# Moving the dilated up-projection under attention, and the experts' weight subtractions from GpSimd to VectorE past routing, with 16-token marks

## The chip, the cores and the metric

One core of one Trainium2 chip. The metric is the time of one execution on the device in microseconds (us): the median of three runs of the same program. One further execution is taken by the hardware profiler, and all rows below come from it. Engines are written PE (TensorE, with PEld for its weight loads), DVE (VectorE), ACT (ScalarE), POOL (GpSimd) and SP (SyncE, which only issues transfers).

## What is computed

A stack of three layers over 512 tokens of 1024 features. The first block has an input projection, sparse attention (NSA) with three branches, dilated attention, two gates that merge them, and PEER, a layer of 16,384 small experts of which each token uses 128. Two hybrid layers with a feed-forward network follow; the change doesn't touch them. The part that matters, shortened:

```python
y_nsa = nsa_attention(...)
y_dil = dilated_attention(...)
gm = sigmoid(mg).reshape(B, S, 2, D)             # mg = h @ w_in[:, gate columns]
merged = gm[:, :, 0] * (y_nsa @ w_up_nsa) + gm[:, :, 1] * (y_dil @ w_up_dil)
x = x + merged @ w_o
# PEER: per token and head the 16 best of 128 keys in each of two halves, then the
# 16 best of the 256 sums; idx = e1 * 128 + e2 names an expert, g its softmax weight
a = einsum('cd,chkd->chk', xt, u[idx])
act = gelu(a) * g
x = x + einsum('chk,chkd->cd', act, v[idx])
```

## The kernel before

All products are of f32 data. A weight page (`WS.load`, 128 x 1024 f32, 512 KB) comes from DRAM on SP's queue into `wr`, is rounded by ACT into `wh` (L99), and `wl = wr - wh` is taken by `self.eng` (L100), VectorE or GpSimd. Each product is then three matmuls (`mm3`, L186 to L188): high by high, high by low, low by high. `wr`, `wh` and `wl` have three buffers each. Eight 128-column pieces make a page.

The order on each engine is worked out by a planner that simulates the program. It may move an instruction ahead of others on its engine unless an edge forbids that. `issue_after(ins)` puts what is traced in its block behind `ins` on the same engine; `keep_in_program_order` puts an instruction behind the one traced before it on its engine. While `self.pinned` is set, the matmuls of the expert loop stay in the traced order.

**Block 1.** `block1` projects the input, runs dilated attention (`dilated`, result `ydh`, `ydl`), normalises the heads (`head_norm`), transposes queries and keys (`to_fm`), compresses keys (`compress`) and runs `nsa`. The gates (`wmg`, 16 column tiles of one page each, evacuated by `evg` to `sg` and written to DRAM as `sig_d`) are traced after `nsa`, but the planner fills PE with them during it. The list `self.hold` says behind which ACT instruction the cast of each of their pages may run: the first four behind the last split of the keys (`start`), twelve behind softmax rows (`self.exps`) spread evenly. A held page has its subtraction on GpSimd. After that come the dilated up-projection `wupd` (2 pages, `ev1`, which loads the gate back from DRAM and writes `m`), the NSA up-projection `wupn` (4 pages, `ev2`) and the output projection `wo1`.

**PEER.** `peer` runs 128 experts' columns in two loops. Each "expert" e of the U loop is one page: 24 matmuls over 384 tokens into one bank, a GELU on ACT, and a transfer to DRAM (`a_d`, L1315) or, from e = RES on, a resident tile (`ares`, L1311). The remaining 128 tokens (TG) are served by gathering their 128 rows of u and of v one by one (`gather`: an indirect transfer issued by GpSimd, L1399, and a row product on VectorE, L1411 for u, L1425 for v).

Beside the U loop, generators are advanced by credits per expert. First `route` finds the experts of the tokens on VectorE: RT_C credits per expert. A tile of 128 tokens costs 41 credits, the whole 164 and a last RT_D. For each tile after the first, `finish` transposes its result on PE; it stands inside the next tile's work, after head h = 6 of the key search. After routing `build_g` builds the weights `g` of all 128 x 384 pairs: `marks` makes on VectorE four f16 tiles of TB tokens (`e1` L1555, `e2` L1557, two `og` L1561), PE multiplies them (L1578), ACT scales (L1580) and SP writes them to `g_d` (L1583). BG_C credits per expert are given to it, one for each yield. NU_C rows per expert are gathered during routing, during `build_g` and after it. In the U loop `wu.eng` is always GpSimd.

The V loop takes the experts in the order RES to 127, then from 0 up to RES: the product of activation and `g` (`at` or `ar` with `gt`, L1334), its split (`ah` L223, `al` L224) and 24 matmuls, with NV_C rows per expert beside it. Subtractions alternate between VectorE and GpSimd there.

Of the kernel before, what the change touches and what calls it, by code (L numbers as in the profile page):

```python
# [20 lines left out]
P = 128  # L21
S = 512
# [56 lines left out]
class WS:  # L79
# [7 lines left out]
    def load(self, p):  # L87
        if p not in self.have and p < self.ap.shape[0]:
# [6 lines left out]
            with ExitStack() as es:  # L95
                if self.b.hold:
                    es.enter_context(self.b.tc.issue_after(self.b.hold.pop(0)))
                    eng = nc.gpsimd
                nc.scalar.copy(hi, raw)  # L99
                eng.tensor_tensor(lo, raw, hi.bitcast(F32), OP.subtract)  # L100
# [15 lines left out]
class Builder:  # L116
# [705 lines left out]
    def to_fm(self, dst, src, scale=None):  # L822
# [6 lines left out]
        else:  # L829
            nc.scalar.mul(dst, p, scale)  # L830
# [4 lines left out]
    def block1(self):  # L835
# [81 lines left out]

        def ev1(t, p):
            nc.scalar.activation(zn[:, t, 8:12].rearrange("p h d -> p (h d)"), p[:, 0:256], AF.Copy,
                                 scale=r4[:, t:t + 1])  # L920
# [23 lines left out]
        for i in range(4):  # L944
            self.to_fm(qT[:, i], lambda t: zn[:, t, 2 * i:2 * i + 2].rearrange("p h d -> p (h d)"), 0.125)
        for i in range(2):
# [4 lines left out]
            for g in range(2):  # L951
                for u in range(2):
                    r = slice(u * 64, u * 64 + 64)
                    start = self.split(kT[0][r, 2 * i + g], kT[1 + u][r, 2 * i + g], p[g * 64:g * 64 + 64])
        self.compress(fs, kcT, vcm)
        ezn.close()

# [15 lines left out]
        m = sp.tile([P, KD, S], F32, name="m")  # L973
        mh = sp.tile([P, KD, S], F32R, name="mh")
        ml = sp.tile([P, KD, S], F32R, name="ml")

        def ev1(c, p):
            t = sp.tile([P, S], F32, tag="gt", name="gt", bufs=3)
            nc.sync.dma_start(t, sig_d[8 + c])
            nc.vector.scalar_tensor_tensor(m[:, c], t, 1.0, p, OP.add, OP.mult)  # L980
# [7 lines left out]
        self.lin(WS(self, self.a["wupd"]), 2, KD, (ydh, ydl), ev1)  # L988
# [22 lines left out]
    def compress(self, fs, kcT, vcm):  # L1011
        tc, nc = self.tc, self.nc
        with ExitStack() as es:
# [27 lines left out]
            nc.scalar.activation(ha, ph[:, 0:256], AF.Gelu_apprx_tanh)  # L1041
# [29 lines left out]
            nc.any.tensor_copy(vcm.rearrange("p g d -> p (g d)"), pv[:, 0:128])  # L1071

# [160 lines left out]
    def peer(self, src):  # L1233
# [5 lines left out]
        g_d = [self.dp.tile([P, NB, 16, NG], F32, tag=f"g_d{e}", name=f"g_d{e}") for e in range(8)]  # L1239
# [40 lines left out]
        for e in range(P):  # L1280
            if e == RES:
                assert routed and next(gen, None) is None
                gen = None
                ap = self.pool(es, "ares")
            wu.eng = nc.gpsimd
# [18 lines left out]
            for k in range(KD):  # L1304
                if routed and gen is not None and k in (2, 6) and credit >= 1.0:
                    next(gen, None)
# [494 lines left out]
```

## Time and profile before

| | |
|---|---|
| median of 3 runs | 3681.76 us (3679.64 to 3682.37) |
| the profiled execution | 3670.07 us |
| its span | 3668.3 us |
| PE busy in the span | 3497.4 us (95%) |
| DVE busy | 2303.4 us (63%) |
| ACT busy | 1397.4 us (38%) |
| POOL busy | 1111.2 us (30%) |

Matmuls are pipelined, and a busy PE is not PE at its peak: how far it is from its floor is read from the pace of its instructions. A window row gives the stretch, its length and, for each engine in the order PE, PEld, DVE, ACT, POOL, the busy time with the count of instructions that touch the stretch; then the granted share of PE's clock (1.00 is the upper of its two levels, 2.4 GHz), the busy share of the transfer engines and what they moved in GB/s. A waits row says who waited for whom, with the total in us, how often, and the longest. A row of a line gives the shortest, middle and longest duration in ns and the first and last start in us from the span's start. Block 1 lasts to about 584 us, the U loop from 634 to 1280, the V loop from there to 1876.

### The profile page before, as it was taken

What the parts mean: (1) busy time and instruction counts of PE and PEld (TensorE: products, weight loads), DVE (VectorE), ACT (ScalarE), POOL (GpSimd) and SP (SyncE); (2) the same over time, 40 slices, a digit from 0 to 9 for tenths busy, and PEclk for the clock granted to TensorE, in tenths of its full rate; (3) what the DMA queues carried; (4) which work ended last, traced back from release to release, by engine and by line L of the source; (5) the groups of instructions that cost most, each with busy time, mean ns of one, the idle gap of its engine ahead of it and who ended that gap; (6) DMA issues with size and microseconds to landing.
All of it is one profiled execution on the core that took longest, in us unless ns stands there. A gap on an engine that the chain in (4) does not pass through costs nothing.

```text
span 3668.3 us, 46596 instructions
## 1 busy us (share of the span) xinstructions
PE 3497.4 (95%) x17784; PEld 2968.8 (81%) x17784; DVE 2303.4 (63%) x3583; ACT 1397.4 (38%) x2159; POOL 1111.2 (30%) x637
## 2 busy tenths in 40 slices
PE   9979999999999899999999999999999999999998
PEld 7856668998999799888888768878887867778886
DVE  5354454999999699999975544554326363464433
ACT  5534433434665233323333443342223344233221
POOL 1002101666667786666620000231101000131100
PEclk9979999999999999999999999999999999999999
DMA  3212143565888999999952323433333333443332
GB/s 129 96 39 92 55 155 100 185 200 194 295 294 296 328 332 352 351 339 348 340 204 88 131 98 127 158 124 97 109 96 112 115 105 103 158 144 103 96 120 75
DMA packets 229016, 631.25 MB, mean 172 GB/s; under 512 B 22644, under 2 KB 57144, under 8 KB 228792
## 3 DMA queue, kind: packets, MB, share of 16 engines
q1 hardware_dynamic: 191928, 494.04, 39.9%
q0 software_dynamic: 36864, 134.23, 10.2%
q8 instruction: 139, 2.28, 0.3%
q14 instruction: 85, 0.70, 0.1%
HBM read 542.20 MB, written 85.98 MB: 171 GB/s over the span
## 4 chain that ended last, share of the span: by engine, by line
PE 71%; DVE 19%; issue 4%; DMA 2%; ACT 2%; POOL 1%; SPq 1%; ACTq 0%; DVEq 0%; POOLq 0%
PE ps L186 17%; PE ps L188 17%; PE ps L187 17%; PE v L186 3%; PE v L187 3%; PE v L188 3%; DVE og L1561 3%; PE o L415 2%; DVE nr L1411 2%; DVE e L1555 2%; PE s L392 2%; DMA wr<-in_pv 1%; PE tp L409 1%; DVE av L1425 1%; ACT wh L99 1%
## 5 line engine op out<-in xcount | busy, mean ns | idle before, releaser
L99 ACT CAST wh<-wr 128x1024 fp32r<-128x1024 f32 x599 | 626.6, 1050 | 1097.7 <-PE ps L187 741.2
L186 PE MATMUL ps<-hnh,wh 128*128 128x512 f32 (+1 forms) x2616 | 979.7, 378 | 16.2 <-ACT hnh L316 11.3
L188 PE MATMUL ps<-hnh,wl 128*128 128x512 f32 (+1 forms) x2616 | 978.4, 374 | 16.1 <-POOL wl L100 16.1
L187 PE MATMUL ps<-hnl,wh 128*128 128x512 f32 (+1 forms) x2616 | 976.7, 373 | 0.1
L100 POOL TENSOR_TENSOR wl<-wr,wh 128x1024 fp32r<-128x1024 f32 x215 | 562.5, 2618 | 699.7 <-ACT wh L99 592.4
L100 DVE TENSOR_TENSOR wl<-wr,wh 128x1024 fp32r<-128x1024 f32 x384 | 478.3, 1246 | 400.1 <-ACT wh L99 387.2
L186 PEld LDWEIGHTS ps<-hnh,wh 128*128 128x128 f32 x2616 | 498.1, 191 | 85.6 <-ACT hnh L316 12.2
L188 PEld LDWEIGHTS ps<-hnh,wl 128*128 128x128 f32 x2616 | 495.9, 190 | 87.5 <-POOL wl L100 19.6
L187 PEld LDWEIGHTS ps<-hnl,wh 128*128 128x128 f32 x2616 | 496.4, 190 | 67.0 <-DVE hnl L320 2.0
L186 PE MATMUL v<-ah,wh 128*128 128x384 f32 x1024 | 349.8, 342 | 44.9 <-ACT wh L99 44.7
L187 PE MATMUL v<-al,wh 128*128 128x384 f32 x1024 | 345.4, 338 | 0.0
L186 PEld LDWEIGHTS v<-ah,wh 128*128 128x128 f32 x1024 | 193.1, 189 | 57.2 <-ACT wh L99 56.4
L188 PE MATMUL v<-ah,wl 128*128 128x384 f32 x1024 | 228.3, 336 | 0.0
L1411 DVE SCALAR_TENSOR_TENSOR nr<-nr,xt 128x1024 f32<-128x1024 f32 x128 | 210.3, 1658 | 13.5 <-DMA nr<-in_ur,gx 13.5
L1425 DVE SCALAR_TENSOR_TENSOR av<-nr,na,av 128x1024 f32<-128x1024 f32 x127 | 211.4, 1665 | 1.6
L187 PEld LDWEIGHTS v<-al,wh 128*128 128x128 f32 x1024 | 193.3, 189 | 0.0
L675 POOL TENSOR_TENSOR sg<-sg,bcs 128x512 f32<-128x512 f32 x44 | 75.7, 1720 | 374.2 <-ACT sg L674 373.9
L1399 POOL DMA_INDIRECT nr<-in_ur,gx x128 | 176.0, 1375 | 39.7 <-issue 13.1
L188 PEld LDWEIGHTS v<-ah,wl 128*128 128x128 f32 x1024 | 182.9, 188 | 0.9 <-POOL wl L100 0.6
L625 POOL TENSOR_TENSOR gc<-gc,gy 128x512 f32<-128x512 f32 x16 | 24.2, 1513 | 522.6 <-DMA wr<-in_wb 237.8
L223 ACT CAST ah<-at 128x384 fp32r<-128x384 f32 x112 | 57.1, 512 | 328.0 <-DVE at L1334 224.6
L1399 POOL DMA_INDIRECT nr<-in_vr,gx x128 | 161.1, 1259 | 40.3 <-issue 19.0
(490 smaller groups left out, 5534.4 us busy)
## 6 DMA issues: line engine op xcount, KB each, us to landing
wr<-in_pu SPq DMA_DIRECT2D x128, 512.0 KB
wr<-in_pv SPq DMA_DIRECT2D x125, 512.0 KB
wr<-in_wgu SPq DMA_DIRECT2D x88, 512.0 KB
g_d<-gs SPq DMA_DIRECT2D x64, 384.0 KB
gt<-g_d SPq DMA_DIRECT2D x32, 768.0 KB
wr<-in_wgate SPq DMA_DIRECT2D x48, 512.0 KB
wr<-in_wdn SPq DMA_DIRECT2D x44, 512.0 KB
a_d<-ga SPq DMA_DIRECT2D x56, 384.0 KB
```

The source lines that it names most:

```text
L99: nc.scalar.copy(hi, raw)
L100: eng.tensor_tensor(lo, raw, hi.bitcast(F32), OP.subtract)
L186: self.pe(nc.tensor.matmul(out, w[0], x[0], start=start, stop=False))
L187: self.pe(nc.tensor.matmul(out, w[0], x[1], start=False, stop=False))
L188: self.pe(nc.tensor.matmul(out, w[1], x[0], start=False, stop=stop))
L392: nc.tensor.matmul(s[:, 0:n], q[:, t * P:n], k[:, 0:n], start=i == 0, stop=False)
L415: nc.tensor.matmul(o[j * 64:j * 64 + 64, b * P:S], heads[j][1](b), pts[j], start=first and b == 0, stop=last and b == NT - 1)
L675: nc.gpsimd.tensor_tensor(t, t, bc, OP.mult)
L1399: i = nc.gpsimd.indirect_dma_start(out=w[:], out_offset=None, in_=self.a[src], in_offset=bass.IndirectOffsetOnAxis(ap=self.near_i[:, j:j + ...
L1411: nc.vector.scalar_tensor_tensor(u, u, 1.0, xts[group[j]], OP.mult, OP.mult, accum_out=a[:, j:j + 1])
L1425: nc.vector.scalar_tensor_tensor(av, w, a[:, j:j + 1], av, OP.mult, OP.add)
L1561: nc.vector.tensor_tensor(o, e1, two(gT[:, i, tt]), OP.mult)
```

## The change

In block 1 the gate columns are packed so that those of the dilated branch come first. Their eight tiles are followed by the dilated up-projection, then by the eight tiles of the NSA gates; `m` moves to a pool that is open from before `nsa`, and `ev1` has its own two buffers `sd`. The list of holds names instructions from earlier on: `marks` holds ACT's last `zn` copy, the tanh of `gf`, the four `qT` copies, the last key split and the GELU of `compress`. There are seven such holds and eleven behind softmax rows, 18 for 18 pages.

In `peer` the subtraction of the U pages is VectorE's once routing is done. TB is 16, with two yields for each 16 tokens. `g_d` is laid out by groups of EG = 4 experts, in 12 blocks of 32 tokens: a write is 512-byte pieces, a read of `gt` one run of 6144 bytes per partition. Twenty experts are resident instead of 16. `build_g` may go on past RES. `finish` moves into the next tile's candidate search, and the row products of u are kept in program order. The credits are set anew.

```diff
             with ExitStack() as es:
-                if self.b.hold:
-                    es.enter_context(self.b.tc.issue_after(self.b.hold.pop(0)))
+                h = self.b.hold.pop(0) if self.b.hold else None
+                if h is not None:
+                    es.enter_context(self.b.tc.issue_after(h))
                     eng = nc.gpsimd
...
+            if t == NT - 1:
+                marks.append(i.ins)
...
-                nc.scalar.activation(gf, gf, AF.Tanh, scale=0.5)
+                marks.append(nc.scalar.activation(gf, gf, AF.Tanh, scale=0.5).ins)
...
-        self.compress(fs, kcT, vcm)
+        marks.append(i_split)
+        marks.append(self.compress(fs, kcT, vcm))
         ezn.close()
+        m = self.pool(er, "ym", side="right").tile([P, KD, S], F32, name="m")
...
-        self.hold = [start] * 4 + [self.exps[i * len(self.exps) // 12] for i in range(12)]
-        self.lin(WS(self, self.a["wmg"]), KD, 16, hn, evg)
+        self.hold = [marks[i] for i in (0, 0, 1, 3, 6, 6, 7)] + [self.exps[i * len(self.exps) // 11] for i in range(11)]
+        wmg = WS(self, self.a["wmg"])
+        self.lin(wmg, KD, KD, hn, lambda c, p: evg(KD + c, p))
+
+        def ev1(c, p):
+            t = gp.tile([P, S], F32, tag="sd", name="sd", bufs=2)
+            nc.sync.dma_start(t, sig_d[KD + c])
+            nc.vector.scalar_tensor_tensor(m[:, c], t, 1.0, p, OP.add, OP.mult)
+        self.lin(WS(self, self.a["wupd"]), 2, KD, (ydh, ydl), ev1)
+        self.lin(wmg, KD, KD, hn, evg)
         self.lin_tags = "bc"
...
-        self.lin(WS(self, self.a["wupd"]), 2, KD, (ydh, ydl), ev1)
         self.lin(WS(self, self.a["wupn"]), 4, KD, (ynh, ynl), ev2)
...
-        g_d = [self.dp.tile([P, NB, 16, NG], F32, tag=f"g_d{e}", name=f"g_d{e}") for e in range(8)]
+        g_d = [self.dp.tile([P, 16 // EG, NB, EG, NG], F32, tag=f"g_d{e}", name=f"g_d{e}") for e in range(8)]
...
             if e == RES:
-                assert routed and next(gen, None) is None
-                gen = None
-                ap = self.pool(es, "ares")
-            wu.eng = nc.gpsimd
+                assert routed
+                ap = self.pool(e2, "ares", side="right")
+            wu.eng = nc.vector if routed else nc.gpsimd
...
-                nc.sync.dma_start(gt, g_d[e // 16][:, :, e % 16:e % 16 + EG])
+                nc.sync.dma_start(gt, g_d[e // 16][:, e % 16 // EG])
...
-                nc.vector.scalar_tensor_tensor(u, u, 1.0, xts[group[j]], OP.mult, OP.mult, accum_out=a[:, j:j + 1])
+                self.tc.keep_in_program_order(
+                    nc.vector.scalar_tensor_tensor(u, u, 1.0, xts[group[j]], OP.mult, OP.mult,
+                                                   accum_out=a[:, j:j + 1]))
...
-                    if h == 6 and last is not None:
-                        finish(*last)
...
+                    if h == 4 and last is not None:
+                        finish(*last)
                     yield 1.5
...
+                    if h % 8 == 4 and h + 4 < TB:
+                        yield 1
                 if t0 + TB == NG:
                     for i in range(8):
-                        nc.sync.dma_start(g_d[i][:, tb], gs[:, 16 * i:16 * i + 16])
+                        nc.sync.dma_start(g_d[i][:, :, tb],
+                                          gs[:, 16 * i:16 * i + 16].rearrange("p (q e) t -> p q e t", e=EG))
...
-TB = 8
+TB = 16
-NB = 8
+NB = 12
-RES = 112
+RES = 108
-RT_D = 8.0
-RT_C = 3.2
-BG_C = 0.85
-NU_C = (0.4, 0.7, 2.0)
+RT_D = 14.0
+RT_C = 2.9
+BG_C = 0.78
+NU_C = (0.3, 1.15, 2.0)
```

## Rows read from the trace of the kernel before

**Rows 1.** The page's chain that ended last, shares of the span by engine

```profile
PE 71%; DVE 19%; issue 4%; DMA 2%; ACT 2%; POOL 1%; SPq 1%; ACTq 0%; DVEq 0%; POOLq 0%
```

**Rows 2.** Windows: an expert, an expert with a step of marks, a projection

```profile
637.96:642.12 4.16, 4.16 (x26) 4.16 (x26) 4.16 (x31) 2.83 (x3) 2.40 (x1) 1.00 0.01 2
...
926.50:931.65 5.15, 5.15 (x41) 4.99 (x41) 5.05 (x6) 3.51 (x4) 3.96 (x3) 1.00 0.88 285
...
520.00:540.00 20.00, 20.00 (x88) 16.13 (x87) 14.47 (x20) 6.58 (x9) 0.00 (x0) 1.00 0.42 142
```

**Rows 3.** Windows: busy us of PE PEld DVE ACT POOL, clock, DMA, GB/s

```profile
633.76:759.04 125.28, 125.28 (x747) 125.19 (x745) 125.04 (x558) 53.58 (x76) 75.77 (x35) 1.00 0.56 185
759.04:889.43 130.39, 118.14 (x660) 117.32 (x658) 129.53 (x344) 45.36 (x66) 85.02 (x39) 0.93 0.58 191
889.43:1182.35 292.92, 285.73 (x2114) 274.17 (x2113) 288.58 (x270) 179.49 (x208) 204.63 (x96) 1.00 0.81 285
1182.35:1280.17 97.82, 80.18 (x410) 76.02 (x409) 59.86 (x74) 24.91 (x36) 77.19 (x46) 0.93 0.93 328
...
1417.44:1876.00 458.56, 416.76 (x2319) 404.86 (x2319) 419.17 (x380) 140.93 (x193) 287.38 (x172) 0.99 0.93 336
```

**Rows 4.** TensorE's waits in U: total us, times, longest

```profile
PE rt L1459 <- DVE em L1527: 12.2, 3, 6.4
...
PE pg L1578 <- DVE og L1561: 5.6, 15, 0.6
...
PE ps L188 <- POOL wl L100: 16.1, 11, 2.7
```

**Rows 5.** Mark operations by line: count, busy us, mean ns, idle before

```profile
L1561 DVE TENSOR_TENSOR og<-e,gT 128x1024 f16<-128x1024 f16 x96 | 115.7, 1207 | 3.6
...
L1555 DVE TENSOR_TENSOR e<-ior,eT 128x1024 f16<-128x1024 f16 x48 | 68.2, 1422 | 0.7
...
L1557 DVE TENSOR_TENSOR e<-ior,eT 128x1024 f16<-128x1024 f16 x48 | 44.1, 920 | 0.0
```

**Rows 6.** Timeline at 918 us: start, us, instruction

```profile
918.38 2.87 POOL L100 TENSOR_TENSOR wl<-wr,wh 128x1024 fp32r<-128x1024 f32 x1 [3.06 <-ACT wh L99]
...
918.93 2.87 DVE L1555 TENSOR_TENSOR e<-ior,eT 128x1024 f16<-128x1024 f16 x1
...
922.51 0.69 DVE L1557 TENSOR_TENSOR e<-ior,eT 128x1024 f16<-128x1024 f16 x1
```

**Rows 7.** VectorE lines: ns min/median/max, first and last start; idle, times

```profile
L1518 DVE TENSOR_TENSOR oh<-fx,ior x8: 1208/1226/2829, 684.5 to 865.5; 128x2048 f16<-128x2048 f16 x8
...
L1411 DVE SCALAR_TENSOR_TENSOR nr<-nr,xt x128: 1195/1215/3950, 716.3 to 1414.8; 128x1024 f32<-128x1024 f32 x128
...
  DMA nr<-in_ur,gx: 13.5, 4
...
L100 DVE TENSOR_TENSOR wl<-wr,wh x13: 1218/1225/1228, 500.4 to 572.1; 128x1024 fp32r<-128x1024 f32 x13
```

**Rows 8.** DMA totals, 889 to 1183 us, then 1305 to 1417 us

```profile
DMA packets 26020, 83.77 MB, mean 285 GB/s; under 512 B 2896, under 2 KB 2896, under 8 KB 25995
...
DMA packets 13641, 39.74 MB, mean 355 GB/s; under 512 B 1208, under 2 KB 4280, under 8 KB 13632
```

**Rows 9.** Last mark matmul and first product with `gt`, by line

```profile
L1578 PE MATMUL pg<-og,e x768: 217/218/233, 890.5 to 1179.1; 128*128 128x128 f16 x192
...
L1334 DVE TENSOR_TENSOR ar<-ar,gt x16: 543/590/2859, 1206.1 to 1282.2; 128x384 f32<-128x384 f32 x16
```

**Rows 10.** ScalarE's waits in V, 1417 to 1876 us

```profile
ACT ah L223 <- DVE at L1334: 209.0, 33, 7.3
```

**Rows 11.** Block 1: two windows, GpSimd's timeline

```profile
229.00:281.00 52.00, 27.98 (x101) 15.39 (x100) 43.89 (x86) 19.54 (x35) 4.28 (x3) 0.61 0.17 59
...
500.00:520.00 20.00, 17.72 (x69) 14.19 (x70) 13.78 (x19) 4.12 (x6) 0.00 (x0) 0.91 0.63 194
...
280.31 7.04 POOL L100 TENSOR_TENSOR wl<-wr,wh 128x1024 fp32r<-128x1024 f32 x3 [40.73 <-issue]
```

More of the change, by code (lines that the diff above doesn't have):

```diff
@@ L829, in to_fm @@
         else:
-            nc.scalar.mul(dst, p, scale)
+            return nc.scalar.mul(dst, p, scale).ins
     def tok_rope(self, t):
@@ L916, in ev0 @@
             nc.scalar.activation(zn[:, t, 0:8].rearrange("p h d -> p (h d)"), p, AF.Copy, scale=r4[:, t:t + 1])
+        marks = []
         def ev1(t, p):
-            nc.scalar.activation(zn[:, t, 8:12].rearrange("p h d -> p (h d)"), p[:, 0:256], AF.Copy,
-                                 scale=r4[:, t:t + 1])
+            i = nc.scalar.activation(zn[:, t, 8:12].rearrange("p h d -> p (h d)"), p[:, 0:256], AF.Copy,
+                                     scale=r4[:, t:t + 1])
+            if t == NT - 1:
+                marks.append(i.ins)
             nc.vector.tensor_scalar(vv[:, t], p[:, 256:512], r4[:, t:t + 1], None, OP.mult)
@@ L944, in block1 @@
         for i in range(4):
-            self.to_fm(qT[:, i], lambda t: zn[:, t, 2 * i:2 * i + 2].rearrange("p h d -> p (h d)"), 0.125)
+            marks.append(self.to_fm(qT[:, i], lambda t: zn[:, t, 2 * i:2 * i + 2].rearrange("p h d -> p (h d)"), 0.125))
         for i in range(2):
@@ L953, in block1 @@
                     r = slice(u * 64, u * 64 + 64)
-                    start = self.split(kT[0][r, 2 * i + g], kT[1 + u][r, 2 * i + g], p[g * 64:g * 64 + 64])
-        self.compress(fs, kcT, vcm)
+                    i_split = self.split(kT[0][r, 2 * i + g], kT[1 + u][r, 2 * i + g], p[g * 64:g * 64 + 64])
+        marks.append(i_split)
+        marks.append(self.compress(fs, kcT, vcm))
         ezn.close()
+        m = self.pool(er, "ym", side="right").tile([P, KD, S], F32, name="m")
         def evg(c, p):
@@ L968, in block1 @@
         self.lin_tags = "b"
-        self.hold = [start] * 4 + [self.exps[i * len(self.exps) // 12] for i in range(12)]
-        self.lin(WS(self, self.a["wmg"]), KD, 16, hn, evg)
+        self.hold = [marks[i] for i in (0, 0, 1, 3, 6, 6, 7)] + [self.exps[i * len(self.exps) // 11] for i in range(11)]
[7 more added lines that the diff above has]
+        self.lin(wmg, KD, KD, hn, evg)
         self.lin_tags = "bc"
         sp = self.pool(es, "b1o")
-        m = sp.tile([P, KD, S], F32, name="m")
         mh = sp.tile([P, KD, S], F32R, name="mh")
         ml = sp.tile([P, KD, S], F32R, name="ml")
[L977 to L980, printed above, removed]
         def ev2(c, p):
@@ L1040, in compress @@
             ha = sp.tile([P, 256], F32, name="ha")
-            nc.scalar.activation(ha, ph[:, 0:256], AF.Gelu_apprx_tanh)
+            gelu = nc.scalar.activation(ha, ph[:, 0:256], AF.Gelu_apprx_tanh).ins
             pt = self.ps(name="pt")
@@ L1071, in compress @@
             nc.any.tensor_copy(vcm.rearrange("p g d -> p (g d)"), pv[:, 0:128])
+        return gelu
     def dilated(self, proj, mkb, ydh, ydl):
@@ L1305, in peer @@
                 if routed and gen is not None and k in (2, 6) and credit >= 1.0:
-                    next(gen, None)
+                    if next(gen, None) is None:
+                        gen = None
                     credit -= 1.0
@@ L1318, in peer @@
         self.pinned = False
+        assert gen is None or next(gen, None) is None
         vp = self.near_p = self.pool(e2, "peer3", side="right")
@@ L1729, in pack_first @@
     arrays["wkvc"] = pack_fm(w, [512 + r(128), 640 + r(128), np.concatenate([1280 + r(24), np.full(104, -1)])])
-    arrays["wmg"] = pack_fm(w, col_tiles(base + 2304, 2048))
+    arrays["wmg"] = pack_fm(w, col_tiles(base + 3328, 1024) + col_tiles(base + 2304, 1024))
     pe = np.zeros((P, 2, 16), f)
```

## The prediction

> **What bounds the kernel now.** I read the chain of waits first: 71% of the span is TensorE and 19% VectorE [rows 1]. So the question in each stretch is how far TensorE runs above its own floor. The floor comes from a clean expert: 24 matmuls of 384 columns in 4.16 us. An expert that also carries one step of marks (16 small f16 matmuls) takes 5.15 us, so a step of marks costs 1.0 us [rows 2]. The windows of the expert loops are then counted against that floor [rows 3]. The first is 28 experts (116.5 us) plus three rounds of key scores, 72 matmuls, 8.6 us: nothing is lost. The second is 27 experts, 112.3 us of 130.4: 18.1 lost. The third is 56 experts and 48 steps, 233.0 + 48 = 281 of 292.9: 11.9 lost. The fourth is 17 experts, 70.7 of 97.8: 27.1 lost. The last 96 experts of the second loop, V, have 399.4 of 458.6: 59.2 lost. The first loop, U, thus takes 646.4 us with a floor of 589.1: 57.3 us to be had.
>
> The waits of TensorE in these windows say what ends last [rows 4]: the transposes of `finish` wait for `em` from VectorE in the second, the mark matmuls for VectorE in the third, the `wl` halves for GpSimd in the fourth. VectorE is busy 288.6 of 292.9 us in the third window, and GpSimd 77.2 of 97.8 in the fourth [rows 3].
>
> **The change part by part. U loop, subtractions.** In the third window the 192 mark operations took 68.2 + 44.1 + 115.7 = 228.0 us [rows 5]. Alone, such an operation takes 0.69 us; one that meets GpSimd's subtraction took 2.87 us and ended just after it [rows 6]. At 0.69 the 192 would have taken 132: some 95 us of VectorE's time were this meeting. The change moves the subtraction past routing to VectorE (1.22 us there [rows 7]), so GpSimd keeps only its gathers. The marks grow to 2048 elements, 1.22 us when undisturbed by the like-sized f16 operation of routing [rows 7], that is 2.45 us for 8 tokens. Per expert VectorE then has 0.78 x 2.45 = 1.91 of marks, 1.15 x 1.22 = 1.40 of row products [rows 7] and 1.22 of subtraction: 4.53 us, their small followers not counted. TensorE needs 4.16 + 0.78 x 1.0 = 4.94. TensorE becomes the bound of this stretch, by a narrow margin.
>
> By the credits in the code routing issues 164 + 14 credits at 2.9 per expert, so 62 experts instead of 54; 48 yields at 0.78 are 62 experts instead of 57, so the marks end in expert 123, not 110, and 4 experts are left instead of 17. Floors: routing 62 x 4.16 + 8.6 = 266.5, marks 62 x 4.16 + 48 = 305.9, the rest 16.6.
>
> What stays lost. Routing: VectorE is busy through both of the first windows [rows 3], and each of the three `finish` comes up to 6.4 us before its tile is there [rows 4]. It now stands 11 credits later, 11/2.9 x 4.16 = 16 us, and fewer credits per expert let VectorE catch up: 1 us stays of 18.1. Marks: I keep the 11.9 us of today, between 0 (VectorE's 4.53 always fits) and 35 (each expert 0.57 late, the 59.2/96 = 0.62 per step that V loses today at a like load of VectorE and transfers). The last four: 1 us instead of 27.1. Together 14 us lost of 57.3: **minus 43**.
>
> Transfers in this stretch: 62 weights of 0.524 MB, 72 gathered rows of 0.524, `g_d` 25.2 and `a_d` 9.0, together 104 MB. Today 83.8 MB go there at 285 GB/s; the busiest long stretch that kept TensorE at its floor ran at 355 [rows 8]. At 355 the 104 MB need 294 us and at V's 336 [rows 3] 311: about the floor of 306. This is why I do not take the floor itself. The Trainium skill, in DMA: Bandwidth & Descriptors, section Where 436 GB/s comes from, puts what HBM gives a core at about 358 GB/s, and the trace's 355 agrees. By it the transfers of this stretch would need 292 us and would not bind.
>
> `g_d` in 512-byte pieces: 96 issues of 256 KB in place of 64 of 384 KB, four pieces per partition. No row shows such a write. Its price lies between nothing (the same bytes) and that of splitting; the nearest row is the 1305 to 1417 stretch, where 768-byte reads are in the mix and 355 GB/s is kept [rows 8]. I take nothing and let the 35 us above hold the rest. Their issues stand on SyncE ahead of weight loads; the cover is two pages of prefetch, some 8 us.
>
> **U to V.** Today 27 us lie between the last mark matmul (1179.1) and the first product with `gt` (1206.1) [rows 9], most of it the write of `g_d` and the load of `gt` behind it; 17 experts cover it. Now four and a half experts are left, 19 us. So V starts 8 us late, plus the restart: **plus 10** (0 if the planner's order hides it, 18 if first weights of V also queue behind the waiting `gt` load on SyncE).
>
> **V loop.** ScalarE's next weight cast stands behind `ah`, which waits for the product with `at`: 209 us in 33 waits [rows 10]. Four more resident experts save two `at` loads on each side, 0.8 MB, 2.4 us at 336 GB/s [rows 3]; `gt` comes in one 6 KB run per partition instead of eight of 768 bytes. Its gain is between 0 and, if the whole stretch shortens with 3% of transfer time, 14 us; I take 4, near the lower end, because the 768-byte runs stood in a stretch of 355 GB/s. Together **minus 6**. The row products pinned behind the VectorE instruction before them add nothing where rows have landed: four of 128 waited for one [rows 7].
>
> **Block 1.** From 229 to 281 TensorE is busy 28 of 52 us at a granted clock of 0.61, and GpSimd's first gate subtraction runs at 280.3 [rows 11]: no gate product is free before. Now the first two pages are freed by ACT's last `zn` copy, the third by `gf`, the fourth by the second `qT`. Three pages fit into the hole: 72 matmuls at 20/88 = 0.227 us [rows 2], 16.4 us of work that leaves the attention stretch, where TensorE is bound. The dilated projection, 48 matmuls, moves ahead into the same fill; after attention its start lost 19 of 88 matmuls in 500 to 520 [rows 11], 4.3 us, and that goes. Against it stand three more gate evacuations in VectorE's queue (0.69 each) and perhaps one meeting with a GpSimd subtraction (2.2): 4. **Minus 17**, between minus 21 (no delay) and minus 8 (attention turns out bound by its softmax chains, so that only the projection's remaining 8 us hide). The 16-token `e1`, the moved `m` and the marks themselves issue nothing else.
>
> **Sum**: -43 + 10 - 6 - 17 = -56. The profiled execution ran 3670.1 us (span 3668.3), so 3614 by its own time. The median of the runs shown is 3681.8, and taking the same 56 off gives 3625.
>
> **Rivals.** (a) The marks run at TensorE's floor, because the transfers hold 355 GB/s throughout and each meets its cover: 12 us more, the junction half hidden (5 more), V 8 better: -81, 3601. For it: VectorE's 4.53 under 4.94. Against: 92% of an in-order engine, where today's 98% leaves 11.9 lost. (The limit of the Trainium skill's DMA page, above, leads to this case too.)
> (b) Crowding: transfers and VectorE are both near full, weights land late behind `g_d`, marks lose 35, V gains nothing, block 1 gives 8: -20 + 10 + 0 - 8 = -18, 3664. For it: V today, with 0.62 lost per step at 93% of the transfer engines.
> (c) Slower: a pinned row product that waits for its gather now holds the subtraction of the next weights and the marks behind it on VectorE; before, the subtraction ran on GpSimd. Such a wait cost 13.5/4 = 3.4 us [rows 7]. A third of the 72 rows would cost 24 x 3.4 = 81 us: 3706. It decides from 64 us, 0.9 per row, which eats the gain and 0.2%. Against it: rows are fetched four ahead, about 18 us.
> (d) The change does not do what it says in block 1: the planner still finds no free `wh` buffer or bank for the first pages before 280, and only the 4.3 us are won: 3638.
>
> **How the numbers follow.** Forecast (3605 to 3645) 0.50, (a) 0.17, (b) 0.15, (c) 0.10, (d) 0.08. The range 3590 to 3662 leaves out (c), the outer half of (b) and the lower tail of (a). A measurement of this kernel tells some 0.2%, 7.4 us, from no change: faster is all of the forecast, (a), (d) and two thirds of (b), 0.85; same 0.05; slower 0.10, the case (c).
>
> **What would show it.** Experts past routing at 5.15 or less with a step of marks, mark operations at 1.22 us each and none near 2.9, no `wl` wait for GpSimd; the `em` wait near zero; VectorE about 92% busy there. A hole of about 10 us between the loops. GpSimd's first gate subtraction near 225 instead of 280, and no loss of pace between attention and the projections. Wrong would be: marks stretch above 341 us, row products waiting for gathers more than 60 us in all, or block 1 ending less than 8 us earlier.

## The result and the profile after

The changed kernel takes 3620.73 us (median of four runs, 3614.13 to 3627.08) where the kernel before takes 3680.70 beside it; the ratio is 0.9844, with a 95% interval of 0.9826 to 0.9863. A second set of runs on another chip gave 0.9851 (0.9836 to 0.9865), 3622.12 us against 3674.82. By the ratios that is 55 to 57 us won (by the medians 53 and 60), and the sum on record was 56.

The profiled execution of the changed kernel is the slowest of its four runs, 3627.08 us with a span of 3625.2, and it lies only 43 us below the profiled execution of the kernel before, which was a quick one (3670.07 us where its medians are 3674.8 to 3680.7). Up to V's end the two differ by 39 us. Behind V, where the change has no edit, the time scatters: 1786.9 to 1797.5 us in the fourteen profiled executions of this study. So parts are compared below by the times of their stages, and whole kernels by ratios of medians.

The page's chain that ended last, by engine, answers to [rows 1]:

```profile
PE 86%; DVE 7%; DMA 2%; issue 2%; ACT 2%; SPq 1%; POOL 0%; ACTq 0%; DVEq 0%; POOLq 0%
```

The chain spends 86% on TensorE instead of 71%, and 7% on VectorE instead of 19%: VectorE no longer sets the pace of U. Windows of the expert loops, with the columns of [rows 3]: routing, marks, the last four experts, the gap between the loops, V.

```profile
629.83:897.52 267.69, 267.69 (x1571) 267.58 (x1570) 253.26 (x890) 108.78 (x155) 171.71 (x78) 1.00 0.58 194
897.52:1219.32 321.80, 312.68 (x2257) 302.37 (x2257) 261.76 (x299) 183.98 (x218) 115.71 (x72) 0.98 0.94 319
1219.32:1235.96 16.64, 16.64 (x97) 16.48 (x96) 12.74 (x18) 6.56 (x10) 10.48 (x8) 1.00 1.00 321
1235.96:1248.56 12.60, 0.17 (x1) 0.00 (x0) 6.12 (x8) 3.43 (x6) 4.24 (x3) 0.66 1.03 416
1248.56:1837.11 588.55, 550.01 (x3089) 537.43 (x3089) 540.70 (x539) 190.41 (x266) 377.38 (x227) 1.00 0.92 338
```

Routing holds 62 experts and runs at its floor, 62 x 4.16 + 8.6 = 266.5 us. The marks take 321.8 us against 305.9 (62 experts and 48 steps): 15.9 lost, where [rows 3] lost 11.9. The last four experts take 4.16 us each. U is 606.1 us long in place of 646.4. In the gap of 12.6 us TensorE does nothing while the transfer engines are full, at 416 GB/s. V takes 588.5 us in place of 596.

TensorE's waits from 629 to 1249 us (total us, times, longest) answer to [rows 4]:

```profile
PE v L187 <- ACT ah L224: 12.4, 1, 12.4
PE ps L187 <- ACT wh L100: 3.5, 3, 2.5
PE pg L1590 <- DVE og L1573: 3.0, 2, 2.1
PE ps L189 <- DVE wl L101: 2.6, 4, 0.6
```

The waits for `em` (12.2) and for GpSimd's low halves (16.1) are gone; the largest is now the gap itself. VectorE's lines in the marks (count, busy us and mean ns, idle before) answer to [rows 5] and [rows 7]:

```profile
L1422 DVE SCALAR_TENSOR_TENSOR nr<-nr,xt 128x1024 f32<-128x1024 f32 x71 | 85.9, 1219 | 0.0
L101 DVE TENSOR_TENSOR wl<-wr,wh 128x1024 fp32r<-128x1024 f32 x61 | 74.5, 1221 | 56.6 <-ACT wh L100 56.5
L1573 DVE TENSOR_TENSOR og<-e,gT 128x2048 f16<-128x2048 f16 x48 | 58.3, 1220 | 2.4 <-PE pg L1590 2.4
L1567 DVE TENSOR_TENSOR e<-ior,eT 128x2048 f16<-128x2048 f16 x24 | 29.3, 1221 | 0.2
L1569 DVE TENSOR_TENSOR e<-ior,eT 128x2048 f16<-128x2048 f16 x24 | 29.2, 1218 | 0.0
```

Every mark operation has the 1.22 us that the prediction took for it, and none is near the 2.87 us of the meeting in [rows 6]. VectorE even sits idle 56.6 us, waiting for casts, and is busy 81% of the stretch (261.8 of 321.8 us), not the 92% of the prediction: an expert takes 5.19 us there instead of 4.94, and each operation starts some 80 ns before the one ahead of it has ended, which a sum of durations counts twice. The chain through the gap (start us, us, what) names what fills it:

```profile
1236.03 9.90 DMA gt<-g_d
1245.95 2.03 DVE ar L1344
1248.00 0.52 ACT ah L224
```

It is the load of `gt` behind the last write of `g_d`, the path of [rows 9], now with four experts over it. In block 1, a window before the hole and one over it, with TensorE's wait behind the second, and the value products of dilated attention with their first and last start:

```profile
205.00:251.00 46.00, 45.32 (x228) 34.75 (x227) 12.40 (x27) 16.37 (x48) 9.61 (x7) 1.00 0.23 75
251.20:266.80 15.60, 0.26 (x3) 0.02 (x1) 13.22 (x11) 6.85 (x8) 0.00 (x0) 0.57 0.01 1
...
PE bc L1133 <- issue: 15.6, 1, 15.6
...
L1184 PE MATMUL po<-dpt,vt x96: 272/273/323, 81.1 to 251.2; 128*64 128x128 f32 x96
```

The same wait and the same products in the kernel before:

```profile
PE bc L1124 <- issue: 15.6, 1, 15.6
...
L1175 PE MATMUL po<-dpt,vt x96: 272/273/476, 79.0 to 235.4; 128*64 128x128 f32 x96
```

The hole is still there, 15.6 us as before, only later. TensorE is full from 205 to 251: the three freed gate pages ran there, ahead of the hole, and pushed dilated attention's last value product from 235.4 to 251.2 us. GpSimd's gate subtractions do stand at 212, 218 and 227 us instead of 280 [rows 11]:

```profile
212.43 2.39 POOL L101 TENSOR_TENSOR wl<-wr,wh 128x1024 fp32r<-128x1024 f32 x1
...
217.83 2.40 POOL L101 TENSOR_TENSOR wl<-wr,wh 128x1024 fp32r<-128x1024 f32 x1
...
227.06 2.39 POOL L101 TENSOR_TENSOR wl<-wr,wh 128x1024 fp32r<-128x1024 f32 x1 [6.16 <-ACT wh L100]
```

### The profile page after: what moved, and what is told of

Its sections match the earlier page's. It is cut to its first block, busy times and chain, and to the rows that moved or that the text cites. A ratio compares the mean times of both kernels' runs of the same rounds, so it can differ in the third digit from the quotient of the medians.

```text
span 3625.2 us, 46499 instructions
## 1 busy us (share of the span) xinstructions
PE 3485.5 (96%) x17784; PEld 2963.6 (82%) x17784; DVE 2230.1 (62%) x3551; ACT 1394.6 (38%) x2159; POOL 958.2 (26%) x574
## 4 chain that ended last, share of the span: by engine, by line
PE 86%; DVE 7%; DMA 2%; issue 2%; ACT 2%; SPq 1%; POOL 0%; ACTq 0%; DVEq 0%; POOLq 0%
PE ps L187 22%; PE ps L189 22%; PE ps L188 21%; PE v L187 3%; PE v L188 3%; PE v L189 3%; PE o L416 2%; PE s L393 2%; PE tp L410 1%; ACT wh L100 1%; PE pg L1590 1%; DMA wr<-in_pu 1%; DVE av L1437 1%; DMA wr<-in_pv 1%; PE pss L253 1%
## 5 line engine op out<-in xcount | busy, mean ns | idle before, releaser
L101 DVE TENSOR_TENSOR wl<-wr,wh 128x1024 fp32r<-128x1024 f32 x447 | 561.8, 1257 | 480.8 <-ACT wh L100 469.7
L101 POOL TENSOR_TENSOR wl<-wr,wh 128x1024 fp32r<-128x1024 f32 x152 | 399.0, 2627 | 652.0 <-ACT wh L100 538.7
L1409 POOL DMA_INDIRECT nr<-in_ur,gx x128 | 191.3, 1494 | 229.6 <-DVE nr L1422 207.7
L189 PE MATMUL v<-ah,wl 128*128 128x384 f32 x1024 | 240.6, 337 | 0.0
L1422 DVE SCALAR_TENSOR_TENSOR nr<-nr,xt 128x1024 f32<-128x1024 f32 x128 | 166.7, 1316 | 0.0
```

The costliest lines, as they stand in the source:

```text
L189: self.pe(nc.tensor.matmul(out, w[1], x[0], start=False, stop=stop))
L1409: i = nc.gpsimd.indirect_dma_start(out=w[:], out_offset=None, in_=self.a[src], in_offset=bass.IndirectOffsetOnAxis(ap=self.near_i[:, j:j + ...
L1422: nc.vector.scalar_tensor_tensor(u, u, 1.0, xts[group[j]], OP.mult, OP.mult, accum_out=a[:, j:j + 1]))
```

## The experiments

Times are in us; the ratio is to the kernel before in the same set of runs, with its 95% interval. "U from" is the start of U's first matmul, U and V go to the end of their last, "gap" is the time from the end of one loop's last matmul to the start of the other's first, all from the profiled execution.

| kernel | median | ratio | U from | U | gap | V |
|---|---|---|---|---|---|---|
| before | 3674.8 to 3680.7 | 1 | 633.8 | 646.6 | 0 | 596.0 |
| after | 3620.7 | 0.9844 (0.9826 to 0.9863) | 629.8 | 606.3 | 12.4 | 588.5 |
| after_again | 3622.1 | 0.9851 (0.9836 to 0.9865) | 627.4 | 600.4 | 10.5 | 589.6 |
| u_only | 3633.9 | 0.9884 (0.9858 to 0.9909) | 634.9 | 603.1 | 8.2 | 593.3 |
| b1_only | 3666.7 | 0.9981 (0.9964 to 0.9998) | 625.7 | 649.2 | 0 | 594.2 |
| fill_hole | 3617.4 | 0.9837 (0.9817 to 0.9857) | 620.1 | 602.0 | 11.7 | 589.2 |
| sub_pool | 3648.4 | 0.9919 (0.9901 to 0.9937) | 626.2 | 625.2 | 7.8 | 595.4 |
| sub_dve_only | 3673.1 | 0.9990 (0.9978 to 1.0002) | 635.9 | 650.6 | 0 | 588.3 |
| unpinned | 3652.6 | 0.9934 (0.9914 to 0.9955) | 627.8 | 641.5 | 0 | 587.7 |
| move_pin | 3647.0 | 0.9905 (0.9888 to 0.9922) | 638.0 | 618.7 | 0 | 591.9 |
| finish_early | 3640.6 | 0.9890 (0.9870 to 0.9911) | 626.3 | 615.9 | 13.0 | 591.1 |
| marks_sooner | 3621.2 | 0.9847 (0.9828 to 0.9866) | 630.5 | 606.6 | 0 | 597.8 |
| eg8_fill | 3625.8 | 0.9861 (0.9846 to 0.9877) | 618.6 | 595.1 | 7.8 | 605.9 |
| fill_gd | 3613.7 | 0.9825 (0.9812 to 0.9839) | 621.3 | 595.4 | 7.7 | 599.8 |

### The subtraction and the pin

**sub_pool** puts the one line back:

```diff
-            wu.eng = nc.vector if routed else nc.gpsimd
+            wu.eng = nc.gpsimd
```

> The changed kernel with the weight subtractions of the U loop on GpSimd past routing again; all else as changed. Theory (the meeting of VectorE's mark operations with GpSimd's subtraction was the main loss of U past routing): mark operations of 1.22 us that meet a subtraction take about 2.9 us or more again, VectorE goes from 81% to over 93% busy in the marks, that stretch (321.8 us in the changed kernel) takes 340 to 365 us, and the last experts wait for their low halves on GpSimd; the time rises by 20 to 45 us. Rival (the larger steps and the new credits carry the gain, the meeting was hidden by then): the stretch stays below 330 us and the time within 8 us of the changed kernel.

Measured: 0.9919 against 0.9844 to 0.9851, some 26 us slower, and U 19 to 25 us longer. VectorE's lines in its marks, 894 to 1235 us:

```profile
L1422 DVE SCALAR_TENSOR_TENSOR nr<-nr,xt 128x1024 f32<-128x1024 f32 x74 | 150.8, 2063 | 12.8 <-DMA nr<-in_ur,gx 12.8
L1573 DVE TENSOR_TENSOR og<-e,gT 128x2048 f16<-128x2048 f16 x48 | 88.6, 1851 | 8.8 <-PE pg L1590 8.6
L1567 DVE TENSOR_TENSOR e<-ior,eT 128x2048 f16<-128x2048 f16 x24 | 46.5, 1939 | 0.1
L1569 DVE TENSOR_TENSOR e<-ior,eT 128x2048 f16<-128x2048 f16 x24 | 36.9, 1540 | 1.5 <-PE pg L1590 1.5
```

Beside GpSimd's subtractions each kind of VectorE operation takes longer than in the changed kernel: 74 x 0.84 + 48 x 0.63 + 24 x 0.72 + 24 x 0.32 = 118 us in all. The move pays 74.5 us of VectorE's time for that (61 subtractions, above). TensorE waits for GpSimd's low halves again:

```profile
PE ps L189 <- POOL wl L101: 16.3, 11, 2.5
```

So the theory held: the meeting is real, and moving the subtraction takes it away. The trace tells the two cases apart: of the 73 row products that start in this window, 18 overlap no subtraction and take 1215 ns on the mean, and 55 overlap one and take 2355. Of the 48 `og`, 23 take 1215 ns and the 25 that overlap a subtraction 2436. All four kinds read two tiles from SBUF, and the row product loses most in all. The Trainium skill, in SBUF — State Buffer, section Who interferes with whom, states the rule: a VectorE instruction with two inputs in SBUF contends with a GpSimd instruction that reads SBUF. The 1219 and 2063 ns here agree with it.

**sub_dve_only** is the reverse, that line alone put into the kernel before.

> The kernel before with one line of the change: past routing its weight subtractions run on VectorE. Theory: the 27.1 us of the last seventeen experts go to about 3, and the marks' stretch loses some of its 11.9 us, so U falls from 646 to 612 to 622 us with the routing stretch (18.1 lost) as before; V keeps its 596; the time is 24 to 34 us below the kernel before. Rival (subtraction, row products and marks then crowd VectorE: 0.85 x 2.76 + 0.70 x 1.22 + 1.22 = 4.4 us per expert in an order that is not pinned): the marks' stretch grows by what the last experts win, less than 10 us in all.

Measured: 0.9990 (0.9978 to 1.0002), next to nothing; U is even 4 us longer than before. The rival came out: what the last experts win, 27 us, is lost in the marks. There and up to V, 885 to 1287 us, TensorE waits for VectorE and for casts:

```profile
PE pg L1578 <- DVE og L1561: 15.4, 14, 3.4
PE ps L186 <- ACT wh L99: 11.5, 3, 5.9
```

**unpinned** shows what came out of order; it takes only the pin away from the changed kernel:

```diff
-                self.tc.keep_in_program_order(
-                    nc.vector.scalar_tensor_tensor(u, u, 1.0, xts[group[j]], OP.mult, OP.mult,
-                                                   accum_out=a[:, j:j + 1]))
+                nc.vector.scalar_tensor_tensor(u, u, 1.0, xts[group[j]], OP.mult, OP.mult, accum_out=a[:, j:j + 1])
```

> The changed kernel with the row products of U left to the planner's order, not pinned into the program's. Theory: pinning carries little, since rows are fetched four ahead and no product waits long for its row: within 6 us, with U within 5 us of 606. Rival (pinning is what keeps a row product from standing in the way of a subtraction that TensorE waits for): U 10 us longer or more. The rival of the prediction, that pinned products wait for their gathers, would make this kernel faster by 10 us or more.

Measured: 0.9934, some 32 us slower than the changed kernel, U 35 to 41 us longer. I had called the pin a thing of little weight; it is worth as much as the move. The first 205 us of the marks, changed kernel and then unpinned, a window and the row products in it:

```profile
897.50:1102.50 205.00, 201.06 (x1458) 195.10 (x1456) 174.25 (x197) 115.60 (x138) 73.51 (x46) 0.98 0.95 321
...
L1422 DVE SCALAR_TENSOR_TENSOR nr<-nr,xt x45: 1214/1219/1223, 896.9 to 1096.3; 128x1024 f32<-128x1024 f32 x45
```

```profile
895.00:1100.00 205.00, 177.04 (x1198) 167.57 (x1196) 182.88 (x231) 98.65 (x117) 122.80 (x74) 0.94 1.00 359
...
L1421 DVE SCALAR_TENSOR_TENSOR nr<-nr,xt x71: 1214/1218/1227, 898.1 to 1096.8; 128x1024 f32<-128x1024 f32 x71
...
PE ps L187 <- ACT wh L100: 14.4, 5, 6.3
PE ps L189 <- DVE wl L101: 13.6, 12, 2.6
```

In the same 205 us unpinned does 71 row products where the changed kernel does 45. Each product frees a row buffer, and GpSimd gathers the next row at once. So the transfers are at 359 GB/s with their engines full (share 1.00). The 26 products more also take some 32 us of VectorE's own time ahead of subtractions. TensorE, busy 177 of 205 us, waits 14.4 us for casts and 13.6 us for subtractions over U (3.5 and 2.6 in the changed kernel). How much of the loss is the transfers' and how much VectorE's was not tried apart. Counted from the trace, the row products begun before a given expert of U:

| expert | before | after | sub_dve_only | unpinned | move_pin |
|---|---|---|---|---|---|
| 60 | 19 | 10 | 35 | 13 | 17 |
| 72 | 28 | 22 | 59 | 40 | 26 |
| 84 | 36 | 37 | 83 | 64 | 34 |
| 96 | 44 | 51 | 91 | 85 | 43 |
| 108 | 52 | 62 | 91 | 95 | 51 |

With the subtraction on VectorE and no pin, the planner puts the row products ahead of the steady pace that the credits meant, and all that U holds are done by expert 102. With the subtraction on GpSimd, or with the pin, they stay spread.

**move_pin** tests that: the kernel before with these two edits and nothing else.

> The kernel before with two edits of the change together: past routing its weight subtractions on VectorE, and the row products of U pinned into the program's order. Theory, from the runs with one of the two missing (without the pin all the row products of U, 91 to 95, are done by expert 102 instead of 49 to 56, and their gathers fill the transfer engines in the marks): together they keep the rows evenly spread, the marks' stretch loses 10 to 15 us instead of 43, the last experts lose nothing, and U takes 610 to 622 us of 646: the time is 25 to 36 us below the kernel before. Rival (the larger steps of marks and the lower credits are needed too, because 0.85 x 2.76 + 0.70 x 1.22 + 1.22 = 4.4 us of VectorE per expert in the old order comes in lumps): less than 15 us below.

Measured: 0.9905 (0.9888 to 0.9922), 29 to 41 us by the interval, 28 by the medians; U takes 618.7 us. Its marks, and what follows them up to V:

```profile
890.00:1168.00 278.00, 278.00 (x2097) 270.45 (x2096) 228.97 (x322) 179.12 (x207) 42.99 (x39) 1.00 0.85 299
1168.00:1256.50 88.50, 78.16 (x424) 75.70 (x423) 65.87 (x101) 26.24 (x38) 44.46 (x31) 0.94 1.01 370
```

TensorE is busy all of 278 us: with the old steps of 8 tokens, the marks lose nothing at all. What is left comes behind them, where two rows per expert are gathered and the transfer engines are full. So move and pin belong together: the changed kernel without either is 26 to 32 us slower (sub_pool, unpinned), the move alone wins next to nothing (sub_dve_only), and the two together carry about half of the gain or more, 28 to 35 us. The pin alone in the kernel before was not run. The larger steps and the new credits for the marks are not needed for this part.

### The call of finish

**finish_early** calls `finish` after head 6 of the key search again:

```diff
+                    if h == 6 and last is not None:
+                        finish(*last)
...
-                    if h == 4 and last is not None:
-                        finish(*last)
```

> The changed kernel with the finish of a token tile called where the kernel before calls it, in the key search, 11 credits earlier. Theory: TensorE waits for the expert marks from VectorE again in the routing stretch, 4 to 16 us in all over three tiles, as the 12.2 us of the kernel before; the routing stretch (267.7 us) takes 272 to 284 us and the time rises by as much. Rival (with 2.9 credits an expert instead of 3.2 VectorE is no longer behind, and the place of the call is worth nothing): below 2 us in the routing stretch.

Measured: 0.9890, 14 to 17 us slower. The first 57 experts of its routing and TensorE's waits there:

```profile
626.28:888.80 262.52, 249.51 (x1456) 248.96 (x1455) 247.34 (x884) 102.57 (x145) 160.31 (x71) 0.98 0.52 180
...
PE rt L1472 <- DVE ge L1546: 13.0, 2, 11.8
```

The 13.0 us of busy time that are missing are two waits of the transposes for VectorE. Its first 62 experts take 282.4 us, those of the changed kernel 267.7. Counted by experts 24 to 48 against their floor (24 x 4.16 us and one round of scores, 2.9), the kernel before loses 17.7 us, finish_early 15.4 and the changed kernel 0.4. So the place of the call is worth most of routing's 18.1 us, and the lower credits alone would have left them nearly as they were.

### Block 1

**u_only** is the changed kernel with block 1 as it was, **b1_only** the kernel before with the block 1 part alone.

> The changed kernel with block 1 put back as it was: the gate pages wait for the last key split again, the dilated projection comes after all sixteen gate columns. Theory: nearly the whole gain is in the expert loops, because the first three gate pages now run at about 205 to 250 us, ahead of the hole of 250 to 267 us instead of inside it, and push the last dilated attention product from 235.8 to 250; so this kernel starts its first expert near 633.8 us (629.8 with the edit) and its time is 3 to 8 us above the changed kernel. Rival: the block 1 edit is worth the 17 us of the prediction and the profiled pair hid it behind a chance of that execution; then this kernel is 14 to 20 us above the changed kernel.

> The kernel before with the block 1 part of the change alone. Theory: 3 to 8 us below the kernel before (about 3675), first expert near 629.8 us, hole of TensorE between 250 and 267 us as wide as before. Rival (the predicted term): 17 us below, about 3664. The expert loops should take what they took before (646 us and 596 us).

Measured: u_only 0.9884, 12 to 15 us above the changed kernel, with intervals that overlap a little; b1_only 0.9981 (0.9964 to 0.9998), 7 us below the kernel before. U begins at 625.7 to 630.5 us in the seven executions with the edit alone, mean 627.7, and at 633.8 to 638.0 in the four without it, mean 635.7. So the edit is worth about 8 us: more than my theory had, and half of the 17 predicted. The 8 us were small waits outside the hole: TensorE's idle time ahead of U, added up from the trace, is 47.6 to 48.8 us in the four executions without the edit and 39.3 to 41.1 in the seven with it.

**fill_hole** puts the first three gate columns where the prediction had them, behind the last value product:

```diff
             p = self.ps("lin")
-            for k in range(nk):
-                self.mm3(p, ws.next(), (hi[:, k], lo[:, k]), k == 0, k == nk - 1)
+            with ExitStack() as es:
+                if after is not None and c < n_after:
+                    es.enter_context(self.tc.issue_after(after))
+                for k in range(nk):
+                    self.mm3(p, ws.next(), (hi[:, k], lo[:, k]), k == 0, k == nk - 1)
...
-        self.lin(wmg, KD, KD, hn, lambda c, p: evg(KD + c, p))
+        self.lin(wmg, KD, KD, hn, lambda c, p: evg(KD + c, p), after=self.dil_last, n_after=3)
...
-            nc.tensor.matmul(o[:, blk(b)], vt[:, b, hs], pts[0][:, b], start=True, stop=not two)
+            self.dil_last = nc.tensor.matmul(o[:, blk(b)], vt[:, b, hs], pts[0][:, b], start=True, stop=not two).ins
```

> The changed kernel with one thing more: the 72 matmuls of the first three gate columns are issued on TensorE only after the last value product of dilated attention, so that they fall into the hole of 250 to 267 us instead of ahead of it. Theory (the fill ran ahead of the hole, so its 16 us were only moved): the last dilated value product goes back to about 236 us, the hole is filled, the first expert starts 12 to 16 us earlier than 629.8, and the time falls by 10 to 16 us. Rival (what follows the hole is a chain on VectorE and ScalarE that takes its time from the row sums onward, and the pages sit on the PSUM banks or delay that chain): the first expert moves less than 4 us, and the time stays within 5 us.

The window that answers to the hole, and the matmuls in it:

```profile
237.30:253.00 15.70, 15.70 (x69) 12.54 (x67) 13.34 (x13) 9.42 (x11) 0.00 (x0) 1.00 0.10 33
...
L187 PE MATMUL ps<-hnh,wh 128*128 128x512 f32 x22 | 8.8, 401 | 0.0
L189 PE MATMUL ps<-hnh,wl 128*128 128x512 f32 x22 | 8.7, 396 | 0.0
L188 PE MATMUL ps<-hnl,wh 128*128 128x512 f32 x22 | 8.7, 396 | 0.0
```

The hole is full, 66 gate matmuls at the upper clock where it was granted 0.57, and U begins at 620.1, 8 us earlier than the mean with the edit and 16 earlier than without it; eg8_fill and fill_gd, which have it too, show 618.6 and 621.3. That is nearly the 17 us of the prediction. Filling a hole of 15.6 us won 8, not 15.6, because the three pages no longer cover the small waits around it (TensorE waits 3.6 us for `zn` and 2.7 for `r`, 0.2 and none in the changed kernel): TensorE's idle time ahead of U is 32.0 to 32.8 us in these three. So the start came less early than my 12 to 16 us, and the 10 to 16 us of time did not show: the ratio, 0.9837, cannot be told from 0.9844 and 0.9851. Up to V's end this execution is 14 and 5 us ahead of the two of the changed kernel; behind V it has 4.5 us more than they.

### The gap, the small pieces and V

**marks_sooner** sets BG_C from 0.78 to 0.85.

> The changed kernel with the marks spread less far: 0.85 of a step per expert instead of 0.78, so that they end about five experts sooner, near expert 118, and nine experts are left to cover the write of g_d and its load. Theory (the hole of 12.6 us between the loops, and 2.4 us of half clock behind it, are that write and load with nothing over them; 5 experts of 4.16 us are 20.8 us): the hole goes below 2 us; VectorE then needs 0.85 x 2.45 + 1.40 + 1.22 = 4.70 us per expert against TensorE's 4.16 + 0.85 = 5.01, so the marks' own stretch keeps its loss of about 9 us: 10 to 15 us faster than the changed kernel. Rival: VectorE is the bound in the marks (busy 81% on the mean, but in bunches), and packing them tighter gives the same time back there: within 5 us.

Measured: the gap is gone and the time is the same, 0.9847. The expected 10 to 15 us went into V, 597.8 us instead of 588.5. From the last mark to V, and V's first 43 us:

```profile
1188.40:1237.00 48.60, 43.47 (x239) 42.19 (x237) 34.34 (x53) 14.99 (x22) 24.28 (x16) 0.96 1.02 380
1237.00:1280.00 43.00, 36.55 (x196) 35.27 (x195) 36.41 (x48) 12.07 (x17) 24.31 (x16) 0.96 0.85 322
```

Ahead of V the transfer engines are full at 380 GB/s and TensorE already loses 5 us; another 6 go in V's first 43. The last write of `g_d`, its load, the rows and the weights have to pass here in any case, with a gap or without. Against the changed kernel V is 6.5 us behind after eight experts, 13 after 32 and 9 at its end. Only the first of these is explained here.

**eg8_fill** is fill_hole with EG = 8 and RES = 112, so that `g_d` has pieces of 1024 bytes.

> The kernel with the gate fill behind the last dilated value product, and g_d written and read for eight experts at a time instead of four: 1024-byte pieces instead of 512-byte ones, half as many packets of g_d (25 thousand fewer), and 112 instead of 108 experts whose activations go through memory (0.8 MB more). A 512-byte packet took 27 ns (19 GB/s on one of 16 engines), a 4096-byte one 159 ns (25.7): at some 45 ns for 1024 bytes the writes give back about 25.2 MB x (1/19 - 1/22.7) / 16 = 13 us of transfer time. Theory (from the end of routing to the end of V the transfers set the time: 935 to 940 us and 312.5 MB in five kernels whose holes differ by 12 us): that stretch, 935 us, falls by 6 to 12 us, and the time is 6 to 12 us below the kernel with the fill alone. Rival (VectorE sets V, and the transfer engines are merely busy): 935 us within 3, and the same time.

Measured: 0.9861, about 8 us slower than with the fill alone, where 6 to 12 us less were expected; the intervals meet. U is 7 us shorter and the gap 4, but V is 17 us longer. V with the fill alone, then of eg8_fill:

```profile
1233.78:1822.96 589.18, 552.88 (x3089) 540.30 (x3089) 541.01 (x539) 190.65 (x266) 372.84 (x225) 0.99 0.91 337
```

```profile
1221.51:1827.45 605.94, 558.13 (x3089) 547.35 (x3089) 539.72 (x539) 192.79 (x266) 384.84 (x226) 0.98 0.89 331
```

The theory that the transfers set the whole stretch up to V's end falls: their engines' share in V went down, from 0.91 to 0.89, while V became slower. Its `gt` loads are 1.5 MB and stand ahead of weights on SyncE's queue; that they cause it was not tried apart.

**fill_gd** is fill_hole with `g_d` laid out as before the change, but in the new blocks of 32 tokens, so written in pieces of 2048 bytes and read in twelve of 512:

```diff
-        g_d = [self.dp.tile([P, 16 // EG, NB, EG, NG], F32, tag=f"g_d{e}", name=f"g_d{e}") for e in range(8)]
+        g_d = [self.dp.tile([P, NB, 16, NG], F32, tag=f"g_d{e}", name=f"g_d{e}") for e in range(8)]
...
-                nc.sync.dma_start(gt, g_d[e // 16][:, e % 16 // EG])
+                nc.sync.dma_start(gt, g_d[e // 16][:, :, e % 16:e % 16 + EG])
```

> The kernel with the gate fill behind the last dilated value product, and g_d laid out as in the kernel before: written in pieces of 2048 bytes, read back for four experts in twelve pieces of 512 bytes. This puts the small packets on V's side; the number of gt loads stays as in the changed kernel. Theory (the 512-byte writes cost the marks their last 5 to 7 us and the hole 3, as the run with 1024-byte pieces showed, and what V lost there, 16 us, came of its 1.5 MB loads of gt standing ahead of weights): U near 595 us, hole near 8, V 589 to 596 us, and the time 3 to 8 us below the kernel with the fill alone. Rival (small packets cost as much wherever they stand: 49 thousand of 27 ns on 16 engines, 83 us against 64 in large pieces, are 19 us, and V has less room for them): U near 595, V 600 us or more, and the same time or up to 6 us above.

Measured: U 6.6 us and the gap 4.0 shorter than with the fill alone, V 10.6 longer, which is an exchange: U and the gap came as the theory had them, V as the rival had it. SyncE's queue in V (packets, MB, share of 16 engines), first with the fill alone, then fill_gd:

```profile
q1 hardware_dynamic: 31561, 113.48, 51.6%
```

```profile
q1 hardware_dynamic: 74335, 115.01, 55.5%
```

The same megabytes take 333 us of 16 engines instead of 304 (0.555 x 599.8, 0.516 x 589.2), since 43 thousand packets more are small. So neither layout is free: small pieces cost U 7 and the gap 4, or V 11. At 3613.7 us and 0.9825 (0.9812 to 0.9839) fill_gd is the fastest kernel here; its interval overlaps a little with the two of the changed kernel (0.9826 to 0.9863, 0.9836 to 0.9865), so the 7 to 10 us between them are likely, not certain.

## Why the prediction was right, and where it wasn't

**U loop, -43.** Right: -40 and -46 in the two executions of the changed kernel. Routing fell from 18.1 lost to 1, mostly by the place of `finish` (finish_early). The marks lost 15.9 and 9.9 in the two, where 11.9 was taken. That size is in part luck: it was kept for a VectorE at 92%, but with 2048-byte writes the same marks lose 4.9 (fill_gd), and move_pin loses nothing. The last experts fell from 27.1 lost to nothing. But that the pinned row products "add nothing where rows have landed" failed, and rival (c) had the pin's sign wrong. The step looked at what a product waits for; the question was what an early one does, which takes VectorE's time ahead of subtractions and sets a buffer free, and with it the next gather. No product waits for its row now (idle 0.0 before the 71), and without the pin 30 us of the gain go.

**512-byte pieces, nothing.** Mis-sized: with the fill alone the marks lose 11.6 us, in fill_gd 4.9 and in eg8_fill 4.6, so about 7 us of it were those pieces, and 4 us of the gap. The bracket of 0 to 35 for the marks held them, but the term was not 0. The Trainium skill, in DMA: Bandwidth & Descriptors, section Specifications, gives 512 bytes as the least for line rate; in the trace a 512-byte packet takes 27 ns of its engine and a 4096-byte one 159, so 19 against 25.7 bytes per ns, and the measurement decides.

**U to V, +10.** Right: 12.4 and 10.5 us by the path named, write and load of `g_d`. In the first of the two the granted clock was 0.66 in the gap and 0.96 over V's first 61.5 us, which is 2.4 us more. What the prediction didn't see is that closing the gap wins nothing (marks_sooner).

**V, -6.** The size was right, -7.4 and -6.4, the parts were not. `gt` in one run is worth 10.6 us against twelve pieces of 512 bytes (fill_gd); against the eight of 768 that the change replaced, for which 4 was taken, no run has it alone. And one part was left out: with 1.15 rows per expert instead of 0.7, 91 rows are done when V begins instead of 82. In kernels with V's code of before, V falls with the rows done: 596.0 and 594.2 us at 82 (before, b1_only), 591.9 at 84 (move_pin), 588.3 at 91 (sub_dve_only), as little as the changed kernel. But u_only, with the changed V and 91 rows, needed 593.3. How the 7 us share out between the two and chance is open.

**Block 1, -17.** Mis-sized: about -8. The failed step is "three pages fit into the hole". They were free by then, as predicted (212 to 227 us), but being free they ran at once, ahead of the last value product, and the hole came 15.6 us later. A page freed early is no page placed; with the placement forced (fill_hole) U begins 16 us earlier than without the edit. Block 1 ending less than 8 us earlier was the prediction's own sign of being wrong: it ended 3.9 and 6.4 us earlier in the two executions, 8.0 on the means above. Rival (d) had a price of 4.3 for this and the wrong reason.

The 9 us missing in block 1 were not made up by the other terms. Up to V's end the two executions are 39 and 48 us ahead of the kernel before: 4 and 6 in block 1, 40 and 46 in U, 7 and 6 in V, less 12.6 and 10.7 for the gap. The ratios give 55 to 57. The rest shows in no stage of these pairs and is put down to scatter between executions: the profiled one of the kernel before was a quick one, and the first of the changed kernel its slowest. So the exact agreement of the sum is in part luck.

## What to carry to other kernels

When an engine is relieved or loaded, look at what its other instructions release, not only at what they wait for: a freed buffer starts the next transfer, and a planner may use new freedom to run all of them early. An order that keeps a side stream at an even pace can be worth as much as the work that was moved. And work that is to fill a hole must be tied behind the instruction that opens it; to be free earlier is not enough.

## What the hardware showed

A f32 row product of VectorE, 1219 ns alone, took 2063 ns on the mean over 74 beside GpSimd's subtractions, and f16 mark operations of the same length 1540 to 1939: the meeting is not one of f16 operations only. The transfer engines moved 416 GB/s in a gap of 12.6 us in which TensorE stood still, and 319 to 338 in the long stretches around it; so neither the 355 nor the 358 GB/s of the prediction is the most that they move, over a short stretch at least. Through the hole of 15.6 us TensorE was granted 0.57 of its clock, a mean between its two levels, 1.2 and 2.4 GHz; with the same 15.7 us filled, 1.00.
